# Another order for the hand-over to the feed-forward input product: copied bank first, last normalise later on ScalarE, third group's sums on VectorE

## The chip, the cores and the metric

The kernel runs on one core of a Trainium2 chip. The metric is the device time of one execution in microseconds (us). The engines are named as the profile names them: PE is TensorE (PEld its weight loads), DVE is VectorE, ACT is ScalarE, POOL is GpSimd, SP issues the DMAs. Each engine works off its own list of instructions in the order in which that list was built. A change of 0.2% (1.9 us) is about what a measurement of this kernel can tell from none.

## The reference

One layer of a hybrid encoder block on a sequence of 512 tokens of width 1024, in float32. What matters here is the end of the token-mixing half and the start of the channel-mixing half:

```python
h = _layer_norm(DEEPNORM_ALPHA * h + g1 * mix_out) * ln1_w + ln1_b      # mix_out = mix @ w_out
u2 = _layer_norm(h) * (1.0 + sc2) + sh2
a, bb = jnp.split(u2 @ w_ffn_in, 2, axis=-1)                             # 1024 -> 2 x 2816
ffn = (jax.nn.silu(a) * bb) @ w_ffn_out
h = _layer_norm(DEEPNORM_ALPHA * h + g2 * ffn) * ln2_w + ln2_b
```

So between the product with `w_out` and the product with `w_ffn_in` stand two normalisations of each token, a transposition, and a scale and shift.

## The kernel before

Every float32 product is made of three fast ones: an operand is split into a rounded high part (`hi`, one ACTIVATE on ScalarE) and the rest (`lo`, one subtraction on VectorE), and PE adds hi\*hi, lo\*hi and hi\*lo in one PSUM bank. `split_act` is this pair of instructions.

**End of the token mixing.** `w_out` is applied in four blocks of 128 tokens (`tt` 0 to 3), each in two halves of 512 columns (`hf`). For each half VectorE adds the residual (`h`, L889) and takes statistics (L890). At the end of a block it makes the mean and the inverse root (`ln_fin`, L261 to L266, whose power runs on POOL, L265), applies the first normalisation (`affine`, L271 and L272), takes statistics again (L257) and makes the factors `rn` of the second one. ScalarE then writes the normalised block `un` (L275, two halves). PE transposes `un` in eight pieces (L839), ScalarE applies scale and shift on the way out of PSUM into `ufh` (L843). PE's own order is the order in which the program is written, and later parts of the hand-over are queued by ticks: a tick falls after each column block of `w_out` and after each half of a feed-forward product, and `later(n, f)` runs `f` n ticks on. `mlag` is such a lag, from the end of a block to its transposition.

**The input product of the feed-forward.** The 2 x 2816 columns are worked in 11 groups of 256 columns of each half: the columns of `a` (tile `raw`) and of `b` (tile `rawu`). Group 0 is computed plainly, as eight products ("a" or "b", token half h, contraction half kh). Groups 1 to 10 use a scheme of seven products instead of eight, with sums of weight quarters and sums of token parts. A product (g, n) multiplies one weight part, split into `prod`, with one token part, split into `left[n]`; it is 24 matmuls of 128x256. The token parts `left[1]` and `left[2]` come from the first 256 tokens alone (tt 0 and 1), all others need the last block too (tt 3). The weight sums of a group are four additions of 128x1024 (`sums`, which = 1 to 4; on VectorE for group 1, on POOL for the others). `sums(g, 2)` makes tile `t2`, which is split for product (g, 6). `t2` and `un` share one buffer.

**Banks.** A group has three PSUM banks. Bank z takes product (g, 1). It is copied by ScalarE to `p1` (L965), and then product (g, 2) is added in the same bank, so (g, 2) cannot start before the copy is done. Bank x takes (g, 6), (g, 7), (g, 4), and is read by VectorE between them; bank y takes (g, 5) and (g, 3).

**Who sets the order.** PE and SP run as written. The order on VectorE, ScalarE and POOL is chosen when the kernel is built, by a priority list: `ahead_of_weights()` raises what stands in it. In the list `order`, PE's products stand one after the other; `prepare` writes the splits and sums four products ahead.

Of the kernel before, what the change touches and what calls it, by code (L numbers as in the profile page):

```python
# [15 lines left out]
P = 128  # L16
T = 512
NT = T // P
D = 1024
# [31 lines left out]
def body(ctx, tc, x, c, w_ada, b_ada, w_in, b_gate, lb_logits, norm_w, w_proj_a, g_ln_w, g_ln_b,  # L51
# [29 lines left out]
    def s2(name="s2"):  # L81
        return tmp["s2"].tile([P, 512], F32, name=name, tag="s2")

    def s4(shape, name):
        return tmp["s4"].tile(shape, F32, name=name, tag="s4")
# [188 lines left out]
    def normalise(dst, src, rn):  # L274
        A.activation(dst, src, AF.Identity, bias=rn[:, 1:2], scale=rn[:, 0:1])  # L275
# [525 lines left out]
    def ffn_load(*names):  # L801
        for n in names:
            g = int(n[1:])
            raws[n] = (wp.tile([P, 2048], F32, name="raw", tag="raw") if n[0] == "a" else
                       ua.tile([P, 2048], F32, name="rawu", tag="u")).rearrange("p (k c) -> p k c", k=8)
            c0 = g * 256 + (DFF if n[0] == "b" else 0)
            nc.sync.dma_start(raws[n], wcols(w_ffn_in, c0, 256).rearrange("(k p) c -> p k c", p=P))

    ffn_load("a0", "a1")

# [9 lines left out]
    def left_split(n, src, ts):  # L822
        split_act(src, left[n][:, 0, :, ts], left[n][:, 1, :, ts])
# [25 lines left out]
    def modulate2_second(tt):  # L849
        ts = slice(tt % 2 * P, (tt % 2 + 1) * P)  # L850
        if tt > 1:
            a11, a12 = ufh[0][:, 0:4, ts], ufh[0][:, 4:8, ts]
            a21, a22 = ufh[1][:, 0:4, ts], ufh[1][:, 4:8, ts]
            if tt == 2:
                left_tile(ua, 8)
                for n in (6, 7, 5, 4, 3):
                    left_tile(ub, n)
            with ahead_of_weights():
                left_split(8, a21, ts)
                left_split(4, a22, ts)  # L860
            s1 = s2("s1").rearrange("p (k t) -> p k t", k=4)
            with tc.high_priority(offset=120):
                V.tensor_tensor(s1, a21, a22, OP.subtract)
                V.tensor_tensor(a21, a11, a21, OP.subtract)
                V.tensor_tensor(a11, s1, a11, OP.subtract)
                left_split(6, a11, ts)
                left_split(7, a21, ts)
                left_split(5, s1, ts)
                V.tensor_tensor(a12, a12, a11, OP.add)
                left_split(3, a12, ts)  # L870
# [4 lines left out]
        for tt in range(2):  # L875
            gemm_t(head[tt][:, 0, :], wo[0], tt, mh, ml, *k)

    mlag = [5, 5, 5, 9]
    for tt in range(NT):
        ht = h1t(tt)  # L880
        bst = sm.tile([P, 2, 6], F32, name="bst")
        for hf in range(2):
            first = hf == 0 and tt < 2
            ps = head[tt] if first else acc_ps().rearrange("p (a b) -> p a b", a=2)
            for i in range(first, 2):
                gemm_t(ps[:, i, :], wo[2 * hf + i], tt, mh, ml)
            with ahead_of_weights():
                sl = slice(hf * 512, (hf + 1) * 512)
                V.scalar_tensor_tensor(ht[:, sl], ht[:, sl], ALPHA, ps.rearrange("p a b -> p (a b)"), op0=OP.mult, op1=OP.add)  # L889
                V.bn_stats(bst[:, hf, :], ht[:, sl])  # L890
        with ahead_of_weights():
            mv, rn = ln_fin(bst)
            affine(ht, mv, rn, l1)
            un = s4([P, D], "un")
            rn = ln_stats(ht)
            for hf in range(2):
                sl = slice(hf * 512, (hf + 1) * 512)
                normalise(un[:, sl], ht[:, sl], rn)

        later(mlag[tt], lambda tt=tt, un=un: modulate2(tt, un))  # L900


    t2s = {}
# [1 line left out]
    def sums(g, which, eng):  # L905

        ra, rb = raws[f"a{g}"], raws[f"b{g}"]
        if which == 1:
            ins = eng.tensor_tensor(ra[:, 0:4], ra[:, 0:4], rb[:, 0:4], OP.add)
        elif which == 2:  # L910
            t2s[g] = s4([P, 4, 256], "t2")
            ins = eng.tensor_tensor(t2s[g], ra[:, 0:4], rb[:, 4:8], OP.add)
        elif which == 3:
            ins = eng.tensor_tensor(rb[:, 0:4], rb[:, 0:4], rb[:, 4:8], OP.add)
        else:
            ins = eng.tensor_tensor(ra[:, 4:8], ra[:, 4:8], t2s[g], OP.add)
        if g == 1:
            tc.keep_in_program_order(ins)

    prods = {}  # L920
    nprod = [0]
# [37 lines left out]
    def collect(g, n):  # L959

        d = part.setdefault(g, {})
        ps = {k: banks.get((g, k)) for k in "xyz"}
        if n == 1:
            d["p1"] = wide(s2("p1"))
            A.activation(d["p1"], ps["z"], AF.Copy)  # L965
        elif n == 6:
            d["v6"] = wide(s2("v6"))
            V.tensor_tensor(d["v6"], ps["x"], d["p1"], OP.add)
        elif n == 2:
            d["sa"] = wide(s2("sa1"))  # L970
            A.activation(d["sa"], ps["z"], AF.Silu)
        elif n == 7:
            d["v67"] = wide(s2("v67"))
            V.tensor_tensor(d["v67"], ps["x"], d["p1"], OP.add)
        if n in (5, 7):
            d["c22"] = d.get("c22", 0) + 1
            if d["c22"] == 2:
                V.tensor_tensor(d["v67"], ps["y"], d["v67"], OP.subtract)
        if n == 4:
            V.tensor_tensor(d["p1"], ps["x"], d["p1"], OP.add)  # L980
            A.activation(d["p1"], d["p1"], AF.Silu)
            if g % 2 == 0:
                hid.append(ua.tile([P, 4, 512], F32, name=f"hid{g // 2}", tag="u"))
            V.tensor_tensor(half(g, 1), d["p1"], d["v67"], OP.mult)
        if n == 3:
            V.tensor_tensor(d["v6"], ps["y"], d["v6"], OP.subtract)
            V.tensor_tensor(half(g, 0), d["sa"], d["v6"], OP.mult)
# [5 lines left out]
    def plain(c, h, kh):  # L993
        n, m = PLAIN[c, h, kh]
        product(0, prods[0, n], left[m], c + str(h), kh == 0, kh == 1, c == "b")
        if c == "b" and kh == 1:
            sa = wide(s2("sa0"))
            A.activation(sa, banks[0, f"a{h}"], AF.Silu)
            if not hid:
                hid.append(ua.tile([P, 4, 512], F32, name="hid0", tag="u"))  # L1000
            V.tensor_tensor(half(0, h), banks[0, f"b{h}"], sa, OP.mult)

    order = [("a", 0, 0), ("a", 0, 1), (1, 1), (1, 2), ("b", 0, 0), ("b", 0, 1),
             ("a", 1, 0), ("a", 1, 1), ("b", 1, 0), ("b", 1, 1), (1, 6), (2, 1), (1, 7), (1, 5), (1, 4), (1, 3)]
    for g in range(2, NG):
        order += [(g, n) for n in ((6, 2, 7, 5, 1, 4, 3) if g + 1 < NG else (6, 2, 7, 5, 4, 3))]
# [1 line left out]
            order[-3] = (g + 1, 1)  # L1008
    ffn_load("b0", "b1", "a2", "b2")
    loaded = 2  # L1010
    eng = {g: V if g < 2 else G for g in range(NG)}
    made = [0]

    def prepare(upto):
        while made[0] < min(upto, len(order)):
            e = order[made[0]]
            made[0] += 1
            if len(e) == 3:
                if e[1] == 0:
                    wsplit(0, PLAIN[e][0])  # L1020
                continue
            g, n = e
            if n in (7, 4):
                sums(g, 3 if n == 7 else 4, eng[g])
            if n == 6 and g == 1:
                sums(1, 1, V)
                sums(1, 2, V)
            wsplit(g, n)
            if n == 1 and g > 1:
                sums(g, 1, eng[g])  # L1030
                sums(g, 2, eng[g])
# [108 lines left out]
```

## Time and profile before

| | |
|---|---|
| median of 3 runs | 954.81 us (954.78 to 955.73) |
| the profiled execution | 956.1 us, of which 954.3 us span |
| PE busy | 917.0 us (96% of the span), 5789 matmuls |
| VectorE busy | 665.6 us (70%) |
| ScalarE busy | 390.5 us (41%) |
| POOL busy | 155.2 us (16%) |
| mean granted clock of TensorE | 0.986 |

Times in the rows are counted from the start of the span. A matmul row shows how long one matmul is in flight; one after the other they start closer together than that. The bracket at the end of a row is the idle time of the engine ahead of it and the instruction that ended it. The granted clock is given as a share: 1.00 is 2.4 GHz, 0.50 is 1.2 GHz.

### The profile page before, as it was taken

The page shows a single profiled execution, that of the slowest core. Times are in us where ns is not written, and L with a number is a line of the kernel's source. Part 1 is how long each engine was busy: PE and PEld are TensorE (multiplying, and loading weights), DVE is VectorE, ACT ScalarE, POOL GpSimd, SP SyncE. Part 2 cuts the span into 40 slices and gives each one's busy share as a digit, 9 for nine tenths or more (in the row PEclk, how much of TensorE's full clock was granted, in tenths as well). Part 3 has the DMA queues.
Part 4 walks back from the last instruction along what each step waited for, and adds up shares of the span by engine and source line. Part 5 has one row for each costly group of instructions (what it writes and reads, how often), then busy time and mean ns, then how long its engine had stood idle before and what let it go on. Part 6 is the DMA issues. An engine that isn't in the chain of part 4 may idle for free.

```text
span 954.3 us, 13895 instructions
## 1 busy us (share of the span) xinstructions
PE 917.0 (96%) x5789; PEld 827.4 (87%) x5789; DVE 665.6 (70%) x962; ACT 390.5 (41%) x520; POOL 155.2 (16%) x103
## 2 busy tenths in 40 slices
PE   5899999999999999999999998989999999999995
PEld 4679998889998888888888998989999999988884
DVE  5756875872138878878327877878888888974337
ACT  4343223321256665665423335534444444541220
POOL 2310020200000000000000011214566554000001
PEclk9899999999999999999999999899999999999998
DMA  9869815362333132222232724022224421842312
GB/s 300 274 193 326 254 45 177 109 199 89 89 89 89 45 89 81 60 81 89 65 112 83 271 90 133 1 89 89 89 89 139 127 89 45 296 146 88 111 45 88
DMA packets 111920, 118.37 MB, mean 124 GB/s; under 512 B 3617, under 2 KB 97906, under 8 KB 111858
## 3 DMA queue, kind: packets, MB, share of 16 engines
q1 hardware_dynamic: 110688, 117.45, 38.3%
q8 instruction: 45, 0.74, 0.3%
q10 hardware_dynamic: 1170, 0.05, 0.1%
q14 instruction: 17, 0.14, 0.0%
HBM read 115.39 MB, written 2.10 MB: 123 GB/s over the span
## 4 chain that ended last, share of the span: by engine, by line
PE 85%; DVE 8%; DMA 2%; ACT 2%; issue 1%; POOL 1%; POOLq 0%; SPq 0%; DVEq 0%; ACTq 0%
PE acc L177 18%; PE acc L175 18%; PE acc L176 18%; PE acc L946 16%; PE sps L946 7%; DVE adaacc L299 2%; PE sps L685 1%; PE sps L318 1%; POOL rn L265 1%; DMA ada<-in_w_ada_dram 1%; DVE h L272 1%; PE sps L729 1%; PE sps L537 1%; PE sps L720 1%; DVE prod L339 1%
## 5 line engine op out<-in xcount | busy, mean ns | idle before, releaser
L150 DVE TENSOR_TENSOR wlo<-raw,whi 128x1024 fp32r<-128x1024 f32 (+2 forms) x101 | 118.7, 1195 | 91.9 <-ACT whi L149 83.2
L946 PE MATMUL acc<-left,prod 128*128 128x256 f32 x1296 | 163.3, 287 | 8.9 <-ACT p L965 4.6
L946 PEld LDWEIGHTS acc<-left,prod 128*128 128x128 f32 x1296 | 160.6, 196 | 9.5 <-ACT p L965 4.8
L149 ACT ACTIVATE whi<-raw 128x1024 fp32r<-128x1024 f32 (+2 forms) x108 | 106.8, 1021 | 148.1 <-PE acc L177 64.8
L175 PE MATMUL acc<-uh,whi 128*128 128x512 f32 x336 | 134.7, 401 | 0.0
L177 PE MATMUL acc<-uh,wlo 128*128 128x512 f32 x336 | 131.3, 391 | 0.0
L176 PE MATMUL acc<-ul,whi 128*128 128x512 f32 x336 | 131.0, 390 | 0.0
L177 PEld LDWEIGHTS acc<-uh,wlo 128*128 128x128 f32 x336 | 63.1, 188 | 13.6
L176 PEld LDWEIGHTS acc<-ul,whi 128*128 128x128 f32 x336 | 63.3, 188 | 12.0
L175 PEld LDWEIGHTS acc<-uh,whi 128*128 128x128 f32 x336 | 63.2, 188 | 11.7
L946 PE MATMUL sps<-left,prod 128*128 128x256 f32 x576 | 72.9, 283 | 0.0
L175 PE MATMUL acc<-whi,uh 128*128 128x256 f32 x256 | 72.7, 284 | 0.0
L177 PE MATMUL acc<-whi,ul 128*128 128x256 f32 x256 | 72.4, 283 | 0.0
L176 PE MATMUL acc<-wlo,uh 128*128 128x256 f32 x256 | 72.4, 283 | 0.0
L265 POOL TENSOR_TENSOR rn<-rn,mhalf 128x1 f32<-128x1 f32 x16 | 18.2, 1136 | 332.6 <-DVE rn L264 332.6
L299 DVE SCALAR_TENSOR_TENSOR adaacc<-ada,cond,adaacc 128x512 f32<-128x512 f32 x82 | 70.2, 856 | 2.0 <-DMA ada<-in_w_ada_dram 0.2
L946 PEld LDWEIGHTS sps<-left,prod 128*128 128x128 f32 x576 | 70.8, 192 | 0.0
L339 DVE TENSOR_TENSOR prod<-raw,prod 128x1024 fp32r<-128x1024 f32 x42 | 56.3, 1340 | 20.6 <-ACT prod L338 20.6
L176 PE MATMUL acc<-wlo,hs 128*128 128x512 f32 x176 | 68.5, 389 | 0.0
L175 PE MATMUL acc<-whi,hs 128*128 128x512 f32 x176 | 68.5, 389 | 0.0
L177 PE MATMUL acc<-whi,hs 128*128 128x512 f32 x176 | 68.5, 389 | 0.0
L338 ACT ACTIVATE prod<-raw 128x1024 fp32r<-128x1024 f32 x42 | 44.3, 1058 | 41.5 <-PE acc L946 16.5
(255 smaller groups left out, 1782.7 us busy)
## 6 DMA issues: line engine op xcount, KB each, us to landing
raw<-in_w_in_dram SPq DMA_DIRECT2D x17, 1024.0 KB, 5.7
ada<-in_w_ada_dram SPq DMA_DIRECT2D x32, 512.0 KB, 9.4
raw<-in_w_in_dram SPq DMA_DIRECT2D x24, 512.0 KB, 5.5
raw<-in_w_ffn_in_dram SPq DMA_DIRECT2D x11, 1024.0 KB, 5.3
rawu<-in_w_ffn_in_dram SPq DMA_DIRECT2D x11, 1024.0 KB, 8.0
raw<-in_w_ffn_out_dram SPq DMA_DIRECT2D x10, 1024.0 KB, 5.1
ada<-in_w_ada_dram SPq DMA_DIRECT2D x8, 1024.0 KB, 6.7
raw<-in_w_proj_b_dram SPq DMA_DIRECT2D x4, 1024.0 KB, 6.5
```

Of the source, the lines that this page charges most:

```text
L149: A.activation(hi[:, k:k + n, :], self.raw[:, k:k + n, :], AF.Copy)
L150: eng.tensor_tensor(lo[:, k:k + n, :], self.raw[:, k:k + n, :], f32(hi[:, k:k + n, :]), OP.subtract)
L175: PE.matmul(ps, ah, bh, start=start, stop=False)
L176: PE.matmul(ps, ah, bl, start=False, stop=False)
L177: PE.matmul(ps, al, bh, start=False, stop=stop)
L265: G.tensor_tensor(rn[:, 0:1], rn[:, 0:1], mhalf[:, 0:1], OP.pow)
L272: V.scalar_tensor_tensor(xa, xa, rn[:, 0:1], wb[:, 1, :], op0=OP.mult, op1=OP.add)
L299: V.scalar_tensor_tensor(a, r, cond[:, k:k + 1], a, op0=OP.mult, op1=OP.add)
L318: PE.matmul(ps[:, o, :], s[:, i * 256 + j * P:i * 256 + (j + 1) * P], ones, start=n == 0, stop=n == len(parts) - 1)
L338: A.activation(hi, src, AF.Copy)
L339: V.tensor_tensor(lo, src, f32(hi), OP.subtract)
L946: PE.matmul(ps[:, i, :], w[:, wi, k, cl], a[:, ai, k, :], start=first and st == (0, 0, 0, 0), stop=last and st == (1, 3, 0, 1), skip_group ...
```

## The change

Seven edits in the hand-over and the first groups:

1. The `a` columns of group 1 are loaded before those of group 0.
2. PE's order starts with (1, 1), and (1, 2) follows after the four products of group 0's first token half, instead of right behind (1, 1).
3. The copy of bank z to `p1` gets the raised priority.
4. The factors of a block's second normalisation are still made at its end, but `un` is written when its tick comes: at the end of the block for blocks 0 to 2, and six ticks later for block 3 (`nlag`).
5. The first two weight sums of group 1 are written in the part of the last block's token sums, with raised priority, instead of right ahead of product (1, 6).
6. The weight sums of group 2 move from POOL to VectorE.
7. A line is gone that kept the sums of group 1 in the written order.

```diff
-    ffn_load("a0", "a1")
+    ffn_load("a1", "a0")
...
                 left_split(4, a22, ts)
+                if tt == 3:
+                    sums(1, 1, V)
+                    sums(1, 2, V)
...
-    mlag = [5, 5, 5, 9]
+    mlag, nlag = [5, 5, 5, 9], [5, 5, 5, 3]
+    rn2, uns = {}, {}
+
+    def pre_modulate(tt):
+        ht = h1t(tt)
+        with ahead_of_weights():
+            uns[tt] = s4([P, D], "un")
+            for hf in range(2):
+                sl = slice(hf * 512, (hf + 1) * 512)
+                normalise(uns[tt][:, sl], ht[:, sl], rn2[tt])
...
-            un = s4([P, D], "un")
-            rn = ln_stats(ht)
-            for hf in range(2):
-                sl = slice(hf * 512, (hf + 1) * 512)
-                normalise(un[:, sl], ht[:, sl], rn)
-
-        later(mlag[tt], lambda tt=tt, un=un: modulate2(tt, un))
+            rn2[tt] = ln_stats(ht)
+        later(mlag[tt] - nlag[tt], lambda tt=tt: pre_modulate(tt))
+        later(mlag[tt], lambda tt=tt: modulate2(tt, uns[tt]))
...
-        if g == 1:
-            tc.keep_in_program_order(ins)
...
-            A.activation(d["p1"], ps["z"], AF.Copy)
+            with ahead_of_weights():
+                A.activation(d["p1"], ps["z"], AF.Copy)
...
-    order = [("a", 0, 0), ("a", 0, 1), (1, 1), (1, 2), ("b", 0, 0), ("b", 0, 1),
+    order = [(1, 1), ("a", 0, 0), ("a", 0, 1), ("b", 0, 0), ("b", 0, 1), (1, 2),
...
-    eng = {g: V if g < 2 else G for g in range(NG)}
+    eng = {g: V if g < 3 else G for g in range(NG)}
...
-            if n == 6 and g == 1:
-                sums(1, 1, V)
-                sums(1, 2, V)
```

**On PE**, at the start of the feed-forward input product. First before, then with the change; `left1` and `left2` are the token parts of the first 256 tokens, `un` is a normalised block, an `acc` or `sps` number is a bank, and each row of 24 is one product (two rows of 12 where transpositions stand between its halves).

```order
L946 MATMUL acc_5068<-left1_4815,prod_5056 128x256 x12
L839 MATMUL sps_5081<-ident_84,un_4891 128x128 x4
L839 MATMUL sps_5090<-ident_84,un_4891 128x128 x4
L946 MATMUL acc_5068<-left1_4815,prod_5056 128x256 x12
L946 MATMUL acc_5068<-left2_4827,prod_5059 128x256 x24
L946 MATMUL acc_5164<-left1_4815,prod_5062 128x256 x24
L946 MATMUL acc_5164<-left2_4827,prod_5065 128x256 x24
L946 MATMUL sps_5217<-left1_4815,prod0_5134 128x256 x12
L839 MATMUL sps_5230<-ident_84,un_5036 128x128 x4
```

```order
L953 MATMUL acc_5065<-left1_4815,prod_5053 128x256 x12
L839 MATMUL sps_5078<-ident_84,un_4926 128x128 x4
L839 MATMUL sps_5087<-ident_84,un_4926 128x128 x4
L953 MATMUL acc_5065<-left1_4815,prod_5053 128x256 x12
L953 MATMUL acc_5136<-left1_4815,prod_5056 128x256 x24
L953 MATMUL acc_5136<-left2_4827,prod_5059 128x256 x24
L953 MATMUL sps_5191<-left1_4815,prod0_5062 128x256 x24
L953 MATMUL sps_5191<-left2_4827,prod0_5133 128x256 x12
L839 MATMUL sps_5228<-ident_84,un_5188 128x128 x4
L839 MATMUL sps_5237<-ident_84,un_5188 128x128 x4
L953 MATMUL sps_5191<-left2_4827,prod0_5133 128x256 x12
L953 MATMUL acc_5065<-left2_4827,prod_5161 128x256 x24
```

Bank z of group 1 is acc_5164 before and acc_5065 with the change: its two products stood next to each other, and now four products and both halves of the transposition of the last block (the second `un`) stand between them. The second transposition stands behind 108 feed-forward matmuls in both versions.

**On ScalarE**, from the last block but one's scale and shift (`ufh1`) on. First before, then with the change; `prod0` are the splits of group 0's `b` weights, `p1` is the copy of bank z, the second kind of `un` row is the last block's.

```order
L843 ACTIVATE ufh1_4509<-sps_5090,mod2_102 128x128
L275 ACTIVATE un_5036<-h11_4468,rn_5042 128x512 x2
L338 ACTIVATE left8_5099<-ufh1_4509 128x4x128
L843 ACTIVATE ufh1_4509<-sps_5090,mod2_102 128x128 x3
L338 ACTIVATE prod0_5134<-rawu_5048 128x1024
L338 ACTIVATE left4_5103<-ufh1_4509 128x4x128
L338 ACTIVATE prod0_5161<-rawu_5048 128x1024
L965 ACTIVATE p1_5189<-acc_5164 128x512
```

```order
L338 ACTIVATE prod0_5062<-rawu_5045 128x1024
L843 ACTIVATE ufh1_4509<-sps_5078,mod2_102 128x128 x4
L843 ACTIVATE ufh1_4509<-sps_5087,mod2_102 128x128
L338 ACTIVATE left8_5096<-ufh1_4509 128x4x128
L843 ACTIVATE ufh1_4509<-sps_5087,mod2_102 128x128 x3
L338 ACTIVATE prod0_5133<-rawu_5045 128x1024
L338 ACTIVATE left4_5100<-ufh1_4509 128x4x128
L973 ACTIVATE p1_5131<-acc_5065 128x512
L275 ACTIVATE un_5188<-h11_4468,rn_5041 128x512 x2
```

`un` of the last block stood ahead of six rows and now stands behind them, the copy of the bank included.

**On VectorE**, behind the first normalisation of the last block (L272). First before, then with the change; `rn_5042` and `rn_5041` are the factors that `un` of the last block needs, `raw_4504` and `rawu_5047` are group 1's weights (L918 is its first sum, L923 its third).

```order
L272 SCALAR_TENSOR_TENSOR h11_4468<-h11_4468,rn_5030,l1p_4473 128x1024
L257 BN_STATS bst_5037<-h11_4468 128x6 x2
L262 BN_AGGR mv_5040<-bst_5037 128x2
L264 TENSOR_SCALAR rn_5042<-mv_5040 128x1
L266 SCALAR_TENSOR_TENSOR rn_5042<-mv_5040,rn_5042 128x1
```

```order
L272 SCALAR_TENSOR_TENSOR h11_4468<-h11_4468,rn_5030,l1p_4473 128x1024
L918 TENSOR_TENSOR raw_4504<-raw_4504,rawu_5047 128x1024
L257 BN_STATS bst_5036<-h11_4468 128x6 x2
L339 TENSOR_TENSOR prod0_5062<-rawu_5045,prod0_5062 128x1024
L262 BN_AGGR mv_5039<-bst_5036 128x2
L923 TENSOR_TENSOR rawu_5047<-rawu_5047 128x1024
L264 TENSOR_SCALAR rn_5041<-mv_5039 128x1
L339 TENSOR_TENSOR left8_5096<-ufh1_4509,left8_5096 128x4x128
L266 SCALAR_TENSOR_TENSOR rn_5041<-mv_5039,rn_5041 128x1
L866 TENSOR_TENSOR s1_5106<-ufh1_4509 128x512
L339 TENSOR_TENSOR prod0_5133<-rawu_5045,prod0_5133 128x1024
```

Three operations of 128x1024 on weights (L918, the split of `prod0_5062`, L923) and one token split have come in between L272 and the last block's factors. Before, the sums of group 1 stood behind the token sums of the last block, and the two splits of `prod0` behind the factors.

## Rows read from the trace of the kernel before

**Rows 1.** Waits of PE from 540 us: total us, times, longest

```profile
PE acc L946 <- ACT p L965: 4.6, 1, 4.6
PE acc L946 <- ACT prod L338: 2.4, 1, 2.4
PE acc L946 <- DVE prod L339: 1.9, 1, 1.9
```

**Rows 2.** Timeline of PE, 565 to 640 us: start, us, instruction, count

```profile
565.05 1.03 PE L839 MATMUL sps<-ident,un 128*128 128x128 f32 x8
...
584.07 1.60 PE L946 MATMUL acc<-left,prod 128*128 128x256 f32 x12
...
586.30 7.43 PE L946 MATMUL acc<-left,prod 128*128 128x256 f32 x60
598.32 4.97 PE L946 MATMUL acc<-left,prod 128*128 128x256 f32 x24 [4.58 <-ACT p L965]
...
615.50 5.92 PE L946 MATMUL sps<-left,prod 128*128 128x256 f32 x48
...
626.16 10.26 PE L946 MATMUL acc<-left,prod 128*128 128x256 f32 x71 [1.93 <-DVE prod L339]
636.26 3.04 PE L946 MATMUL sps<-left,prod 128*128 128x256 f32 x24
```

**Rows 3.** Timeline of ScalarE, 560 to 600 us

```profile
561.50 1.52 ACT L275 ACTIVATE un<-h,rn 128x512 f32<-128x512 f32 x2 [10.05 <-DVE rn L266]
...
592.29 1.52 ACT L275 ACTIVATE un<-h,rn 128x512 f32<-128x512 f32 x2 [4.28 <-DVE rn L266]
...
596.21 0.62 ACT L338 ACTIVATE left<-ufh 128x512 fp32r<-128x512 f32 x1
596.73 1.05 ACT L338 ACTIVATE prod<-rawu 128x1024 fp32r<-128x1024 f32 x1
597.68 0.59 ACT L965 ACTIVATE p<-acc 128x512 f32<-128x512 f32 x1
```

**Rows 4.** Timeline of VectorE and POOL, 611 to 615 us

```profile
611.73 2.89 DVE L865 TENSOR_TENSOR ufh<-s,ufh 128x512 f32<-128x512 f32 x1
...
611.28 2.78 POOL L909 TENSOR_TENSOR raw<-raw,rawu 128x1024 f32<-128x1024 f32 x1 [19.28 <-DVE prod L339]
```

**Rows 5.** Stretches: length, busy us by engine, granted clock, DMA

```profile
48.00:50.00 2.00, 1.82 (x12) 1.72 (x13) 0.65 (x4) 0.46 (x1) 0.00 (x0) 1.00 0.93 265
...
600.00:602.00 2.00, 2.00 (x11) 2.00 (x11) 2.00 (x4) 1.98 (x3) 0.00 (x0) 0.50 0.00 0
...
628.00:630.00 2.00, 2.00 (x12) 2.00 (x11) 0.00 (x0) 0.00 (x0) 0.00 (x0) 0.55 0.00 0
```

**Rows 6.** Timeline of PE at the start of the kernel

```profile
48.18 1.13 PE L318 MATMUL sps<-ones,adaacc 128*128 128x128 f32 x8 [1.66 <-DVE adaacc L299]
```

**Rows 7.** Timeline of VectorE, 588 to 599 us

```profile
588.25 1.28 DVE L272 SCALAR_TENSOR_TENSOR h<-h,rn,l1p 128x1024 f32<-128x1024 f32 x1
589.57 1.29 DVE L257 BATCH_NORM_STATS2 bst<-h 128x6 f32<-128x512 f32 x2
...
591.13 0.16 DVE L264 TENSOR_SCALAR rn<-mv 128x1 f32<-128x1 f32 x1
592.04 0.16 DVE L266 SCALAR_TENSOR_TENSOR rn<-mv,rn 128x1 f32<-128x1 f32 x1 [0.75 <-POOL rn L265]
...
596.74 1.22 DVE L339 TENSOR_TENSOR prod<-rawu,prod 128x1024 fp32r<-128x1024 f32 x1
597.87 0.68 DVE L339 TENSOR_TENSOR left<-ufh,left 128x512 fp32r<-128x512 f32 x1
598.47 0.68 DVE L865 TENSOR_TENSOR ufh<-s,ufh 128x512 f32<-128x512 f32 x1
```

**Rows 8.** Loads of `rawu`: issued 582 to 583.1 us; all in 540 to 650 us

```profile
rawu<-in_w_ffn_in_dram SPq DMA_DIRECT2D x1, 1024.0 KB, 5.4
...
DMA to landing us min/median/max: 5.4/8.3/11.5
```

## The prediction

> **What bounds the kernel now.** I read the page first (PE is busy 96% of the span), then PE's waits from 540 us to the end [rows 1], because a kernel that keeps PE this full can only gain where PE stands still. There are three waits, all in the hand-over: one for the copy of bank z (`p`), two for the weights of one product. The reader is to see that nothing after them makes PE wait, so every microsecond taken from them should come off the end.
>
> PE's timeline [rows 2] gives their full price. Undisturbed, matmuls of this shape start 0.12 us apart (48 of them in 5.92 us, the last one's 0.28 in flight taken off), a product takes 2.88 us, and a set of eight transpositions 0.79 (12 matmuls from 584.07 end at 585.51, PE goes on at 586.30). From 584.07 to 636.26 PE does 13 products and two sets of transpositions: 13 x 2.88 + 2 x 0.79 = 39.0 us of work in 52.2 us. The 13.2 us too many are:
> - 4.8: PE has done 60 matmuls by 593.50 and goes on at 598.32, with product (1, 2), which waits for the copy;
> - 2.0: from 598.32 to 615.50 lie 120 matmuls and a set of transpositions, 15.2 us, but it took 17.2;
> - 4.8: 48 matmuls from 615.50 end at 621.26, and PE goes on in earnest at 626.16, one matmul between, when the weights of (1, 6) are split;
> - 1.6: 71 matmuls from 626.16 should end at 634.68, the next row starts at 636.26.
>
> The second and fourth term are the clock: after each long wait the granted clock is at or near 0.50, that is 1.2 GHz [rows 5] (its second and third row).
>
> Why is the copy late? ScalarE's timeline [rows 3]: the bank was full at about 593.5, the copy runs at 597.68. It stands behind `un` of the last block, which waits for its factors until 592.29, and behind six more rows. The second wait comes from VectorE, which had all sums of group 1 behind the last block's token sums. While POOL ran a sum of group 2, a VectorE operation that takes 0.68 elsewhere [rows 7] took 2.89 [rows 4], and the one behind it likewise.
>
> **The change, part by part.** I lay the durations of the rows into the new order, on the clock of the old trace. Up to 584 us only edits 1 and 4 act. With the loads exchanged, (1, 1) is split where group 0's first weights were. One weight split moves behind L272 of block 0, whose `un` comes some 0.3 us later than 561.50 [rows 3]. It takes 1.52, and PE transposes it at 565.05 [rows 2]: 2 us of cover, so nothing is paid. Without that cover the 0.3 would fall on PE.
>
> *PE from 584.07*, without any wait: half of (1, 1) to 585.51, transpositions of block 2 to 586.30, (1, 1) done at 587.74, the two `a` products at 590.62 and 593.50, the first `b` product at 596.38, half of the second at 597.82, transpositions of block 3, then the other half to 600.05 and (1, 2) to 602.93.
>
> *The copy* (edits 2 and 3). Its bank is full at 587.74 and the next user of the bank is (1, 2) at 600.05. ScalarE reaches the copy before `un`, behind a split that needs L272's end at 589.53 to get its buffer: 589.6 + 0.95 (split) + 0.52 (split) gives 591.1 to 591.6, with the pitches of [rows 3] (596.73 to 597.68 and 596.21 to 596.73). Eight microseconds early: the wait of 4.8 is gone, and with it its 2.0 of clock.
>
> *The last block's factors* (edits 4 and 5). VectorE ends L272 at about 589.5 [rows 7]. Now L918 (1.14 by the pitch 596.74 to 597.87), the statistics (1.2) and the low part of the first `b` weights (1.14) follow: that low part is done at 593.0, and PE needs it with its second matmul at 593.62. L923 takes 1.14 more, then L264 at 594.2; from there to L266 it was 0.91 (591.13 to 592.04), so the factors are there at 595.2, 3.0 later than before. `un` runs 595.3 to 596.9, PE wants it at 597.8. So the later normalise costs nothing, but with 1 us of cover only; beyond that each microsecond is PE's.
>
> *Where the stall goes.* VectorE is the one that is late next. L866 (0.6) runs from 595.2 and the low part of the second `b` weights from 595.8 to 597.0. PE needs that at 596.5: a wait of **0.6**, which moves all that follows to 598.4 (transpositions), 600.6 and 603.5. The product behind (1, 2) is the first with a token part of the last block (`left8`), and its third matmul, at 603.7, needs the low part. Ahead of that VectorE has three operations of 128x1024 and eight of 512 columns from 595.2: 3 x 1.14 + 8 x 0.61 = 8.3, with two dependent steps 8.4, so it starts at 603.6 and ends at 604.3: another **0.6**. The next token part is ready at 606.1 for 607.0. The weights of (1, 6) come out at 611.5, and PE gets there at 615.6: the second wait and its clock are gone, with 4 us of cover. They are early because sums 1 and 2 of group 1 no longer stand behind the last token part, and because POOL is silent (edit 6).
>
> *Edit 6* puts four sums of 1.14, 4.6 us, on VectorE between 614 and 631, where PE takes a new weight every 2.88 us. I laid them out too: VectorE is at the reading of bank x at 619.7 for a need at 621.4, and each later split is 5 to 7 us early. It costs nothing while that holds, and 1.14 for each sum if it did not. Edit 7 only frees what the others use. The loads behind group 1's come some 1.6 us later, since group 0's last split moves back; the first use is 25 us on.
>
> *The sum.* 13.2 lost before, 1.2 lost after: **12.0 us** less. Against the profiled execution's own 956.1 that is 944.1; this execution lay 1.3 above the median of the runs, and against 954.8 it is **942.8 us**.
>
> Do the two short waits cost clock as well? At the start of the kernel PE waited 1.66 us [rows 6], and the granted clock of the stretch behind it is 1.00 [rows 5] (its first row). So I take nothing for it, and 2 us each, as the long waits cost, as the other bound.
>
> **Rivals.**
> *VectorE is later than my sum.* From 589.5 to 604 it stands almost without a gap, so what each of its 20-odd steps takes more is PE's at once. A tenth of 14.5 us is 1.5, and if a wait then grows past those of the start of the kernel, one fall of the clock adds 2.0: 944.3 to 946.3. For it: no row shows this mix in this order. Against: POOL, which slowed VectorE, now has only its short powers here.
>
> *The load of group 1's `b` columns is late.* L918 now stands in VectorE's list ahead of the last statistics and waits for that load, issued between 582 and 583.1; everything in the hand-over queues behind it. The load took 5.4 us, but others of its kind took up to 11.5 [rows 8]. Landing at 588.5 at the latest is 1.0 ahead of 589.5; at 11.5 it would be 594.2 to 594.6, L918 5 us later, PE waiting 5 us more and losing 2.0 of clock: a gain of 5, 949.8. Against: the slow ones were issued while other loads ran, and this one still starts alone. [...]
>
> *The second wait only moves.* If VectorE, with the work that edits 5 and 6 put ahead, brought the weights of (1, 6) more than 4 us later than 611.5, a wait would stay. If all 6.4 us of that wait and its clock stayed: a gain of 5.6, 949.2. Against: the order has that split ahead of all of group 2's sums.
>
> *Slower than before.* PE runs as written, and the transpositions of the last block now hang on an `un` that comes 3 us later by my sum. Everything behind them waits. From 597.8 on each microsecond of `un` is paid in full, and the change turns into a loss once `un` is done more than 12 us after 596.9, at about 610 (with a fall of the clock), slower by 0.2% at 611. That takes a load landing 20 us after its issue, or VectorE at twice its durations throughout. Nothing in rows 8 reaches that; 2 in 100, at 957 or more.
>
> **How the numbers follow.** The forecast, 942.8, holds if the two waits together stay between 0 and 2.5 us: 941.6 to 944.1, chance 0.70. VectorE later: 0.17. The load late: 0.05. The second wait moves: 0.04. Slower: 0.02. Nothing gained, by something I have not seen: 0.02. No wait at all and no clock lost would be 941.6; with 0.3 us for the spread of runs the low end is 941.3. The high end takes in the first rival's upper bound, 946.5, and leaves out about 0.13 above and little below. Faster by over 0.2% (about what a measurement of this kernel can tell from no change): the first four, 0.96; within: 0.02; slower: 0.02.
>
> **What would show it.** In the profile after: PE's wait for the copy is gone, and ScalarE runs the copy near 591.5, ahead of the last `un`. PE has two short waits on VectorE instead, for the second `b` weights near 596.5 and for `left8` near 603.7, each under 1.5 us; no wait ahead of (1, 6); granted clock 1.00 throughout; VectorE's operations between 611 and 618 at their 0.68; (1, 7) ends 12 us earlier than before. I would be wrong in the mechanism if PE waited for the transpositions of the last block, if L918 waited for its load, or if a clock at 0.50 stood after a short wait; wrong in size if VectorE had gaps between 589 and 604.

## The result and the profile after

| | before | after |
|---|---|---|
| median of the runs, us | 954.79 (954.35 to 955.73, 4 runs) | 943.04 (942.47 to 943.88, 4 runs) |
| profiled execution, us | 956.1, span 954.3 | 942.9, span 940.9 |

The ratio of after to before is 0.9876, 95% interval 0.9859 to 0.9893: 11.8 us less.

PE's waits from 540 us to the end, in the view that answers to [rows 1]: the wait for the copy is gone, two short ones on VectorE stand in its place.

```profile
PE sps L953 <- DVE prod L339: 0.6, 1, 0.6
PE acc L953 <- DVE left L339: 0.4, 1, 0.4
```

PE's timeline, which answers to [rows 2]. The reader can count the products: 60 + 25 + 11 matmuls behind the transpositions of block 2, those of block 3, and then 12 + 26 + 46 + 48 + 72 up to the product (1, 5) at 622.91.

```profile
584.52 7.43 PE L953 MATMUL acc<-left,prod 128*128 128x256 f32 x60
591.78 3.16 PE L953 MATMUL sps<-left,prod 128*128 128x256 f32 x25
595.50 1.57 PE L953 MATMUL sps<-left,prod 128*128 128x256 f32 x11 [0.56 <-DVE prod L339]
596.91 1.03 PE L839 MATMUL sps<-ident,un 128*128 128x128 f32 x8
...
599.21 3.28 PE L953 MATMUL acc<-left,prod 128*128 128x256 f32 x26
602.90 5.77 PE L953 MATMUL acc<-left,prod 128*128 128x256 f32 x46 [0.41 <-DVE left L339]
...
614.27 8.80 PE L953 MATMUL acc<-left,prod 128*128 128x256 f32 x72
622.91 3.04 PE L953 MATMUL sps<-left,prod 128*128 128x256 f32 x24
```

The same work, 300 matmuls and one set of transpositions, lies before in [rows 2] between 586.30 and 636.26. Undisturbed it is 300 x 0.12 + 0.79 = 36.8 us. It took 49.96 before and takes 622.91 - 584.52 = 38.39 now: 11.6 us less. (The products are the same but for one half: the stretch starts in the middle of the first product of each order.) The span is 13.4 us shorter; the other 1.8 lie ahead of this stretch, in code that did not change (the last section says where). So below every kernel is read twice: by its median, and by the length of this stretch.

ScalarE's timeline, which answers to [rows 3]: the copy now runs 4.4 us ahead of the last `un`.

```profile
589.31 0.58 ACT L973 ACTIVATE p<-acc 128x512 f32<-128x512 f32 x1
593.74 1.52 ACT L275 ACTIVATE un<-h,rn 128x512 f32<-128x512 f32 x2 [3.85 <-DVE rn L266]
```

VectorE's timeline, which answers to [rows 7]: from L272 on it goes from one operation to the next, with one gap of 0.43 ahead of L266, and the two that PE waits for are the `prod` at 594.23 and the `left` at 602.16.

```profile
587.71 1.22 DVE L918 TENSOR_TENSOR raw<-raw,rawu 128x1024 f32<-128x1024 f32 x1
...
590.04 1.21 DVE L339 TENSOR_TENSOR prod<-rawu,prod 128x1024 fp32r<-128x1024 f32 x1
...
593.55 0.16 DVE L266 SCALAR_TENSOR_TENSOR rn<-mv,rn 128x1 f32<-128x1 f32 x1 [0.43 <-POOL rn L265]
593.62 0.68 DVE L866 TENSOR_TENSOR s<-ufh 128x512 f32<-128x512 f32 x1
594.23 1.22 DVE L339 TENSOR_TENSOR prod<-rawu,prod 128x1024 fp32r<-128x1024 f32 x1
...
602.16 0.69 DVE L339 TENSOR_TENSOR left<-ufh,left 128x512 fp32r<-128x512 f32 x1
```

The stretches around both waits (length, busy us by engine, granted clock), which answer to [rows 5]: PE is idle for about half a microsecond in each, and the clock stays at 1.00.

```profile
592.00:596.00 4.00, 3.44 (x29) 3.24 (x28) 3.57 (x8) 1.52 (x2) 0.83 (x1) 1.00 0.02 5
...
600.00:604.00 4.00, 3.59 (x30) 3.39 (x30) 4.00 (x7) 3.98 (x10) 0.00 (x0) 1.00 0.00 0
```

### The profile page after: what moved, and what is told of

Same layout as the page of the kernel before. It is cut to its first block, busy times and chain, and to the rows that moved or that the text cites. A ratio compares the mean times of both kernels' runs of the same rounds, so it can differ in the third digit from the quotient of the medians.

```text
span 940.9 us, 13895 instructions
## 1 busy us (share of the span) xinstructions
PE 911.9 (97%) x5789; PEld 822.4 (87%) x5789; DVE 663.0 (70%) x966; ACT 390.5 (42%) x520; POOL 144.5 (15%) x99
## 4 chain that ended last, share of the span: by engine, by line
PE 85%; DVE 9%; DMA 2%; issue 1%; ACT 1%; POOL 1%; POOLq 0%; SPq 0%; DVEq 0%; ACTq 0%
PE acc L175 18%; PE acc L177 18%; PE acc L176 18%; PE acc L953 15%; PE sps L953 7%; DVE adaacc L299 2%; PE sps L685 1%; POOL rn L265 1%; DMA ada<-in_w_ada_dram 1%; DVE h L272 1%; PE sps L729 1%; PE sps L537 1%; DVE prod L339 1%; PE sps L318 1%; PE sps L720 1%
## 5 line engine op out<-in xcount | busy, mean ns | idle before, releaser
L953 PE MATMUL acc<-left,prod 128*128 128x256 f32 x1296 | 159.6, 283 | 0.4 <-DVE left L339 0.4
L953 PEld LDWEIGHTS acc<-left,prod 128*128 128x128 f32 x1296 | 157.2, 192 | 0.6 <-DVE left L339 0.6
```

Of the source, the lines that this page charges most:

```text
L953: PE.matmul(ps[:, i, :], w[:, wi, k, cl], a[:, ai, k, :], start=first and st == (0, 0, 0, 0), stop=last and st == (1, 3, 0, 1), skip_group ...
```

## The experiments

The stretch of each kernel, from its own trace (300 matmuls and eight transpositions in each, 36.8 us undisturbed):

| kernel | what it is | stretch, us | median, us |
|---|---|---|---|
| before | | 49.96 | 954.79 |
| after | edits 1 to 7 | 38.39 | 943.04 |
| e1_old_order | after without 1 and 2 | 40.93 | 944.91 |
| e2_pool_sums | after without 6 | 38.36 | 943.90 |
| e3_sums_last | after without 5 and 7 | 44.29 | 949.08 |
| e4_un_early | after without 4 for the last block | 38.31 | 942.63 |
| e5_order_only | before with 1 and 2 | 42.96, and 0.8 behind it | 948.59 |
| e7_first_four | after without 5, 6 and 7 | 38.54, and 1.0 behind it | 944.72 |
| e8_copy_plain | after without 3 | 38.33 | 944.16 |
| e9, e11_two_waits | after, two splits earlier on VectorE | 37.15, 37.04 | 942.31, 942.95 |
| e10_changed | after once more | 38.28 | 942.30 |
| e12_no_pool_pair | before without two POOL sums | 43.99 | 948.37 |

**The first wait: what buys the copy its room.** e1_old_order takes the order of products and loads back:

```
-    ffn_load("a1", "a0")
+    ffn_load("a0", "a1")
-    order = [(1, 1), ("a", 0, 0), ("a", 0, 1), ("b", 0, 0), ("b", 0, 1), (1, 2),
+    order = [("a", 0, 0), ("a", 0, 1), (1, 1), (1, 2), ("b", 0, 0), ("b", 0, 1),
```

> The changed kernel with edits 1 and 2 undone (loads and products in the old order), all else kept. Theory (the order buys the copy its room): bank z is again filled as the fourth product and asked for by the fifth. ScalarE's list then has the first half of the last `un` ahead of the copy, and its factors are not there before about 592 in the time of the trace after. PE waits 2.5 to 4.5 us for the copy and may lose up to 2.0 of clock: 946 to 949.5 us. Rival (the raised priority of the copy, edit 3, would have done it alone): no wait for the copy, 942.5 to 944.

Measured: 944.91 us (ratio to before 0.9884 to 0.9915), between the two ranges: 1.1 under the theory's, 0.9 over the rival's. The trace decides against the rival: the wait for the copy is back, 2.4 us where before had 4.6. PE's timeline of e1_old_order:

```profile
584.08 7.43 PE L953 MATMUL acc<-left,prod 128*128 128x256 f32 x60
593.92 4.48 PE L953 MATMUL acc<-left,prod 128*128 128x256 f32 x24 [2.41 <-ACT p L973]
598.24 1.60 PE L953 MATMUL sps<-left,prod 128*128 128x256 f32 x12
```

The stretches of e1_old_order around that wait; the granted clock is the third number from the end:

```profile
592.00:596.00 4.00, 2.08 (x9) 2.08 (x10) 3.62 (x7) 3.43 (x6) 0.34 (x1) 0.70 0.01 3
596.00:600.00 4.00, 4.00 (x31) 4.00 (x31) 3.62 (x6) 3.57 (x5) 0.00 (x0) 0.88 0.00 0
```

The 24 matmuls behind the wait took 4.48 us where 3.04 is their undisturbed row: 1.4 of clock. From the end of the 60 matmuls to the next one it is 2.6 us (584.08 + 7.20 = 591.28 to 593.92). This kernel has none of the 1.6 us by which after's stretch exceeds 36.8, and these I had not taken off: 2.6 + 1.4 - 1.6 = 2.4, and the stretch is 2.5 longer than after's (1.9 by the median). The mechanism of the theory holds: in the old order edits 3 to 7, the raised copy among them, halve the wait and do not remove it.

e8_copy_plain leaves the copy at its plain priority:

```
-            with ahead_of_weights():
-                A.activation(d["p1"], ps["z"], AF.Copy)
+            A.activation(d["p1"], ps["z"], AF.Copy)
```

> The changed kernel with edit 3 undone: the copy at its plain priority, behind both halves of the last `un`. All else stands in the same order. Theory (the order of the products alone gives the copy its room): copy at about 595.2, bank asked for at 599; no wait; 942.6 to 943.5, the same as the changed kernel. Rival (the raised priority is needed): PE waits for the copy ahead of (1, 2), 945 or more.

Measured: 944.16 us (0.9874 to 0.9906). The copy ran at 595.75, 5.8 later than in after when both are counted from the start of the stretch, and PE did not wait for it. The stretch is after's to 0.1 us, so the 0.7 by which the median lies over the forecast is not in the hand-over. e4_un_early undoes edit 4 for the last block:

```
-    mlag, nlag = [5, 5, 5, 9], [5, 5, 5, 3]
+    mlag, nlag = [5, 5, 5, 9], [5, 5, 5, 9]
```

> The changed kernel with edit 4 undone for the last block (its `un` written with the old lag, so that it stands ahead of the copy and of `left4` on ScalarE). Theory (edit 4 has no price of its own, the copy has 8 us to spare): the copy moves from 589.3 to about 595.3 for a need at 599; VectorE has two operations less ahead of the second `left8`. Same as the changed kernel within 0.6 us: 942.4 to 943.6. Rival (the late `un` is a part of the gain): a wait for the copy returns, 945 or more.

Measured: 942.63 us (0.9857 to 0.989), as the theory has it; the copy at 596.32, no wait for it. With the products in the new order, leaving out edit 3 or edit 4 alone costs nothing that shows in the stretch.

**The order alone.** e5_order_only is the kernel before with the first two edits, the two lines of e1_old_order the other way round.

> The kernel before with edits 1 and 2 alone. The copy stays behind the last `un` on ScalarE, but its bank is asked for by product (1, 2), now six products later. Theory (two separate waits): the wait for the copy and its 2.0 of clock are gone, the wait for the weights of (1, 6) and its clock stay, a gain of 5 to 8: 947 to 950. Rival (VectorE's lateness is the one cause, the order only moves it): the time comes back at (1, 6), gain under 2, 953 to 955.

Measured: 948.59 us (0.9916 to 0.9948), inside the theory's range. Its first half holds: with the order alone, edits 3 and 4 left out, PE no longer waits for the copy. The second half does not: the wait for the weights of (1, 6) did not stay. PE's waits in e5_order_only from 540 us to the end:

```profile
PE acc L946 <- DVE v L968: 1.5, 1, 1.5
PE sps L946 <- DVE prod L339: 1.3, 1, 1.3
PE sps L946 <- ACT prod L338: 0.6, 1, 0.6
PE acc L946 <- DVE v L974: 0.5, 1, 0.5
PE acc L946 <- DVE prod L339: 0.2, 1, 0.2
```

The wait ahead of (1, 6) is down to 0.2 (the last row), though nothing was done about its weights. In its place PE waits 1.9 for the second `b` weights and 2.0 for two readings of bank x (`v`). So what had made the second wait before? POOL's first sum of group 2 starts in this kernel at 616.91, behind a split on VectorE that the new order moved back, and not at 611.28 as in [rows 4]. POOL's timeline in e5_order_only:

```profile
616.91 4.39 POOL L909 TENSOR_TENSOR raw<-raw,rawu 128x1024 f32<-128x1024 f32 x1 [23.88 <-DVE prod L339]
```

**The second wait: what made it.** e12_no_pool_pair is the kernel before without two of POOL's sums; every other engine's list is the same:

```
     def sums(g, which, eng):
+        if g == 2 and which in (1, 3):
+            return
```

> The kernel before, with the first and the third sum of group 2 left out (so group 2's products are made of other numbers). The lists of PE, VectorE, ScalarE and SP are the same as before; only the two POOL sums at 611.28 and 614.15 in the trace of before are gone. Theory (the second wait of before was made by these two sums, which each held one VectorE operation for 2.2 us): the weights of (1, 6) come 4.4 us earlier, the wait of 4.8 shrinks to 0.4, and its 1.6 of clock goes: 6 us less, 948.5 to 950; the wait for the copy and its clock stay. Rival (group 1's late sums on VectorE made it, POOL only lay beside them): 953.5 to 955, the wait ahead of (1, 6) stays above 3.

Measured: 948.37 us (0.9915 to 0.9943), 0.1 under the theory's range and far from the rival's. PE's waits in e12_no_pool_pair from 540 us to the end:

```profile
PE acc L948 <- ACT p L967: 4.3, 1, 4.3
PE acc L948 <- DVE prod L339: 0.2, 1, 0.2
```

Its timeline of PE, at both waits and at the end of the stretch:

```profile
598.11 5.15 PE L948 MATMUL acc<-left,prod 128*128 128x256 f32 x24 [4.34 <-ACT p L967]
...
621.71 8.78 PE L948 MATMUL acc<-left,prod 128*128 128x256 f32 x71 [0.20 <-DVE prod L339]
630.33 3.04 PE L948 MATMUL sps<-left,prod 128*128 128x256 f32 x24
```

The wait for the copy stands, the second wait is 0.2, and the stretch is 6.0 us shorter, the 4.4 and 1.6 that were expected. Group 1's sums are as late in VectorE's list as before; PE hardly waits for them. So the second wait and its clock were made by these two POOL sums; the late sums of group 1 without them leave 0.2. Whether early sums would have taken the wait away in the old order with POOL at work, no run tells.

**The sums.** e2_pool_sums puts group 2's sums back on POOL, all else as after:

```
-    eng = {g: V if g < 3 else G for g in range(NG)}
+    eng = {g: V if g < 2 else G for g in range(NG)}
```

> The changed kernel with edit 6 undone: the sums of group 2 run on POOL again. Theory: VectorE's operations beside a POOL sum go from 0.69 to about 2.9 us, as in rows 4, while PE works on the products from (1, 2) to (1, 6). The weights of (1, 6) have 4 us of cover, a POOL sum slows two VectorE operations by 2.2 each: 0 to 2 us dearer, 943 to 945. Rival (edit 6 is what removed the second wait): PE waits about 4.8 us ahead of (1, 6) and loses 1.6 of clock, 948 to 950.

Measured: 943.90 us (0.9872 to 0.9906), the stretch after's to 0.03. The time is at the low end of the theory's range, but not for the theory's reason: PE does not wait, and no operation of VectorE ahead of the split of (1, 6) is slowed. POOL's first sum starts at 613.33, when the split of (2, 1) is done, and that stands behind the split of (1, 6); the operation held up is POOL's own, as its timeline in e2_pool_sums shows:

```profile
613.33 4.40 POOL L918 TENSOR_TENSOR raw<-raw,rawu 128x1024 f32<-128x1024 f32 x1 [18.48 <-DVE prod L339]
617.81 2.41 POOL L921 TENSOR_TENSOR t<-raw,rawu 128x1024 f32<-128x1024 f32 x1
```

VectorE's timeline of the same kernel beside it, where these operations keep their usual duration (later two splits, at 619.79 and 623.15, take 1.50 instead of 1.22, and PE waits for neither):

```profile
613.11 1.22 DVE L339 TENSOR_TENSOR prod<-rawu,prod 128x1024 fp32r<-128x1024 f32 x1
614.25 1.22 DVE L339 TENSOR_TENSOR prod<-raw,prod 128x1024 fp32r<-128x1024 f32 x1
...
618.70 0.69 DVE L976 TENSOR_TENSOR v<-acc,p 128x512 f32<-128x512 f32 x1 [2.19 <-PE acc L953]
```

e3_sums_last keeps group 2's sums on VectorE and puts group 1's behind the last token parts again:

```
-                if tt == 3:
-                    sums(1, 1, V)
-                    sums(1, 2, V)
...
+        if g == 1:
+            tc.keep_in_program_order(ins)
...
+            if n == 6 and g == 1:
+                sums(1, 1, V)
+                sums(1, 2, V)
```

> The changed kernel with edits 5 and 7 undone: group 1's sums come behind the last block's token parts again, group 2's stay on VectorE. VectorE then has the last block's factors some 2.4 us earlier, and does eight 512-column operations of block 2 ahead of the low part of the second `b` weights. Theory: that low part comes 2.6 us late, so the first of the two short waits grows from 0.6 to about 2.6, while (1, 6), with no POOL beside VectorE, is late by 1 at most: 945 to 948, the upper end if the clock falls. Rival (the place of the sums was the second wait): 4.8 us and 1.6 of clock ahead of (1, 6), 949 to 950.

Measured: 949.08 us (0.993 to 0.9957): the rival's size, at another place than either named. The wait for the second `b` weights is 1.1 and not the theory's 2.6. PE's timeline in e3_sums_last:

```profile
596.44 1.56 PE L952 MATMUL sps<-left,prod 128*128 128x256 f32 x11 [1.11 <-DVE prod L339]
...
623.10 0.38 PE L952 MATMUL acc<-left,prod 128*128 128x256 f32 x1 [2.64 <-ACT prod L338]
624.55 4.52 PE L952 MATMUL acc<-left,prod 128*128 128x256 f32 x23 [1.07 <-DVE prod L339]
628.90 3.04 PE L952 MATMUL sps<-left,prod 128*128 128x256 f32 x24
```

(1, 6) and (2, 1) run without a wait; it is (1, 7) that waits 3.7 us, and 23 of its matmuls take 4.52, with a granted clock of 0.58 in the stretch 624 to 628. Its weights need the third sum of group 1, and VectorE's timeline has three sums of group 2 ahead of that (613.81, 615.54 and 619.48; the third sum of group 1 is the row at 620.62, which has the same line as group 2's third):

```profile
613.81 1.23 DVE L915 TENSOR_TENSOR raw<-raw,rawu 128x1024 f32<-128x1024 f32 x1
...
615.54 1.23 DVE L920 TENSOR_TENSOR rawu<-rawu 128x1024 f32<-128x1024 f32 x1
...
619.48 1.23 DVE L918 TENSOR_TENSOR t<-raw,rawu 128x1024 f32<-128x1024 f32 x1
620.62 1.22 DVE L920 TENSOR_TENSOR rawu<-rawu 128x1024 f32<-128x1024 f32 x1
```

e7_first_four tests that reading: e3_sums_last with the line of e2_pool_sums.

> The changed kernel with edits 5, 6 and 7 undone: group 1's sums last, group 2's on POOL. It is e3_sums_last with group 2's sums taken off VectorE. Theory (in e3_sums_last the weights of (1, 7) were late because VectorE had sums of group 2 ahead of the third sum of group 1): that wait and its clock go, about 5 us, and the wait of 1.1 for the second `b` weights stays: 943.3 to 946, the upper part if POOL's sums hold up VectorE's splits. Rival (the late sums of group 1 alone make (1, 7) late, wherever group 2's are): 948 to 950.

Measured: 944.72 us (0.9884 to 0.9912), as the theory has it: no wait for (1, 7), 1.1 for the second `b` weights, and 0.7 for a reading of bank x that stood behind two splits which POOL held (2.15 and 3.42 us instead of 1.22). So edit 6 costs 4.4 us without edits 5 and 7 (949.08 against 944.72) and nothing with them.

**What is left.** e9_two_waits gives the splits of the `b` weights a higher priority and keeps the fourth sum of group 1 in its place:

```
+        if n in (9, 3) and g == 0:
+            with ahead_of_weights():
+                split_act(s, t[:, 0], t[:, 1])
...
+            if g == 1:
+                tc.keep_in_program_order(ins)
```

> The changed kernel, with the splits of group 0's `b` weights raised in priority and the fourth sum of group 1 kept in its place. On VectorE the low part of the second `b` weights then comes one operation earlier, and the second `left8` two earlier (0.6 and 1.1). Theory (the two short waits of 0.6 and 0.4 and the gaps beside them are what is left to gain): both go, 1.0 to 1.6 us less, 941.4 to 942.2. Rival (the waits move to the next operation that VectorE brings): within 0.4 of the changed kernel.

> The changed kernel itself, to stand beside e11_two_waits on one chip. Both theories: two waits of 0.5 to 0.6 and 0.4 us, 942.5 to 943.8.

> The kernel of e9_two_waits once more, beside the changed kernel. Theory (the 1.2 us that its hand-over is shorter reach the end): 0.6 to 1.4 less than e10_changed. Rival (they are given back later, or lie within the spread of the start of the kernel): within 0.4 of it.

Both waits are gone. PE's timeline of e9_two_waits: the second row now holds all 36 matmuls.

```profile
585.22 7.43 PE L959 MATMUL acc<-left,prod 128*128 128x256 f32 x60
592.49 4.71 PE L959 MATMUL sps<-left,prod 128*128 128x256 f32 x36
...
622.37 3.04 PE L959 MATMUL sps<-left,prod 128*128 128x256 f32 x24
```

The stretch is 37.15 and 37.04, 1.2 shorter than after's. In the times it does not show: 942.31 alone, 0.1 over the theory's range, but beside after on one chip 942.95 against 942.30 (ratios to before 0.9875, interval 0.9858 to 0.9891, and 0.9868, interval 0.9851 to 0.9885), where the theory had 0.6 to 1.4 less. After's four runs there lay between 941.12 and 944.32, so 1.2 us is below what these runs tell. Whether this version is faster stays open.

## Why the prediction was right, and which step was not

*The forecast.* 942.8 us forecast, 943.04 measured; 12.0 us of gain forecast, 11.6 in the stretch. The traces differ by 1.8 us at its start, by which the forecast's places are moved here.

*The first wait.* Shown. The copy was to run at 591.1 to 591.6; it ran at 589.31, which is 591.1 on the old clock. Its wait and the clock behind it are gone; e1_old_order brings about half of the wait back, with a loss of clock, and e5_order_only takes the wait away by the order alone. Edit 3, which the forecast named beside the order, was not needed (e8_copy_plain).

*The second wait.* That it would go was right; **why** was wrong in part. The forecast put it down to the late sums of group 1 and to POOL. e12_no_pool_pair shows that POOL made it: with group 1's sums as late as before and POOL's two gone, the wait is 0.2. Nor are the early sums needed to remove it: e5_order_only, where they are late and POOL works, has 0.2 as well, and there POOL starts 5.6 us later; e7_first_four has none. That the later start is the reason in e5_order_only is read from the two traces and was not tried by itself. What edits 5 and 7 do is to let edit 6 be free (e3_sums_last), and the three together take 1.1 us off what the first four leave (39.5 with the wait behind the stretch, against 38.4). The first four alone bring 10 of the 11.8 us.

*Where the stall goes.* Shown: the second `b` weights were wanted at 594.8 and `left8` at 602.3 (596.6 and 604.1 on the old clock; 596.5 and 603.7 were forecast). The term was sized at 1.2 and measured 38.39 - 36.8 = 1.6: 0.7 and 0.6 at the two places (594.78 to 595.50, 602.33 to 602.90, counting 0.12 for each matmul of the row ahead), and 0.3 in pieces of under 0.1 where one row of PE's timeline goes over into the next, which I had left out.

*Clock.* The forecast took nothing for the short waits, by [rows 6]. The granted clock is 1.00 through both.

*The load.* L918 did not wait. The load of group 1's `b` columns was issued at 580.92 and landed 5.2 us later, 1.6 ahead of L918; 1.0 had been forecast. VectorE's rows start in the order of its list (L918 at 587.71, L257 at 588.84, the split at 590.04, L262 at 591.16, L923 at 591.28). That a late load would have held all behind it was an estimate; a late load was not tried.

*The other rivals.* VectorE took 0.2 longer than laid out from the end of L272 to the factors (587.79 to 593.71, 5.9 for 5.7), and 0.3 longer from the same start to the end of the second `left8` (587.79 to 602.85, 15.1 for 14.8), not 1.5. The transpositions of the last block did not wait: `un` ended at 595.26 and PE came at 596.91. That is 1.6 us of cover with the wait ahead of it; the forecast had 1 without that wait.

*The edits do not add up.* The order is worth 6.2 us alone and 2.5 with the others there; edit 6 nothing or minus 4.4; edits 3 and 4 show nothing one by one, and 4.2 together on top of the order alone (43.7 for e5_order_only with what lies behind its stretch, 39.5 for e7_first_four). So one edit can hide waits that another would also have hidden.

## What to carry to other kernels

When two engines slow each other, look at when the slower one is released and take its work away alone, with all other lists unchanged, before putting the wait down to the list of the engine that is late. An edit that moves work onto the engine that feeds PE is judged by what stands behind it in that engine's list: the same sums were free in one order and cost 4.4 us in another. Compare kernels by the length of the stretch that the change touches, with the same instructions at both ends, when the medians scatter as much as the effect.

## What the runs showed of the hardware

**VectorE and POOL shut each other out of these additions.** I had taken [rows 4] as a slowing. It is waiting. POOL's sum of 128x1024 takes 2.41 us by itself (e2_pool_sums at 617.81), and a VectorE subtraction of 0.68 that begins beside it ends 0.56 behind POOL's end: L865 began at 611.73, POOL's sum ended at 614.06, L865 at 614.62. Without the POOL sum the same instruction took 0.68, as VectorE's timeline in e12_no_pool_pair shows:

```profile
611.69 0.68 DVE L865 TENSOR_TENSOR ufh<-s,ufh 128x512 f32<-128x512 f32 x1
```

The other way round it is the same: in e7_first_four POOL's first sum began at 612.58, VectorE had operations of this kind one behind the other up to 616.99, and the sum took 6.67, that is 2.3 beyond VectorE's end. POOL's timeline in e7_first_four:

```profile
612.58 6.67 POOL L915 TENSOR_TENSOR raw<-raw,rawu 128x1024 f32<-128x1024 f32 x1 [20.58 <-DVE prod L339]
```

The last two of VectorE's rows in that time:

```profile
614.63 1.22 DVE L339 TENSOR_TENSOR prod<-raw,prod 128x1024 fp32r<-128x1024 f32 x1
615.77 1.22 DVE L339 TENSOR_TENSOR prod<-rawu,prod 128x1024 fp32r<-128x1024 f32 x1
```

Not every operation of VectorE is held: `v` at 618.70 in e2_pool_sums, which reads a bank (`acc`), takes its 0.69 while POOL's sum runs from 617.81 to 620.22. So in these rows one of the two waits; what makes it wait no run shows. Which of them comes next when both have work queued they do not settle: in e7_first_four POOL waited through four operations of VectorE in a row, in the kernel before it waited for the one that ended at 611.80 and went ahead of L865.

**PE's clock by the wait ahead of it.** Waits of 0.6 and 0.4 (after), 1.1 (e7_first_four, e3_sums_last) and 1.5 (e5_order_only, ahead of its (1, 7)) were followed by matmuls at the undisturbed pitch to 0.1 us (11 took 1.57 behind the 0.6, 1.58 and 1.56 behind the two of 1.1, where 1.48 is undisturbed; 46 took 5.77 behind the 0.4, for 5.68; 24 took 3.11 behind the 1.5, for 3.04). Behind 2.4 us (e1_old_order) 1.4 us were lost, behind 2.6 and 1.1 in short order (e3_sums_last) 1.6. Behind 0.6 and 1.3 in short order (e5_order_only) the granted clock was 0.70 in the stretch 600 to 604: 11 matmuls took 2.71 us where 1.48 is undisturbed. In columns: at 0.50 in the kernel before, 16 matmuls of 256 columns from 598.69 on took 3.62 us, the last one 0.42 of it in flight, so they started 0.213 apart, 1.2 columns per ns. At 1.00 they start 0.120 apart, and those of 512 columns 0.227 (23 starts from 530.82 to 535.81), so 256 columns more take 0.107 us, 2.4 per ns. These two rates are what the trace shows of the 1.2 and 2.4 GHz named with the clock above.

**The start of the kernel scatters.** The instructions up to 540 us are the same in all of these kernels, and yet the loads of `h`, which they share, were issued from 521.37 on before, 519.51 after and 517.88 in e10_changed. The distance is still there when PE comes to the transpositions of block 2, at 585.51, 583.72 and 581.99. The granted clock from 20 to 40 us was 0.77, 0.91 and 1.00 in these three traces. That stretch in before:

```profile
20.00:40.00 20.00, 16.64 (x77) 14.14 (x76) 14.24 (x21) 6.16 (x10) 6.41 (x3) 0.77 1.08 359
```

In after:

```profile
20.00:40.00 20.00, 15.90 (x79) 12.96 (x78) 14.53 (x22) 7.79 (x12) 5.88 (x3) 0.91 1.08 360
```

And in e10_changed, the same kernel as after:

```profile
20.00:40.00 20.00, 15.94 (x87) 13.36 (x88) 16.07 (x24) 8.69 (x12) 7.20 (x4) 1.00 1.08 360
```

That is 3.5 us between executions that no edit made, and 1.6 of it between two of one kernel; most of the single edits here are worth less. That the clock of the start makes the distance is not tried: the two only go together in these three traces.
